# Hybrid decoder layer on one core: squares of the second x tile on two engines, meta rows scaled on GpSimd, third-last write finished on chip

## The chip, the cores and the metric

The kernel runs on 1 core of one Trainium2 chip. The metric is the device time of one execution in microseconds (us); of several executions the median is given. Engine names are those of the profile: PE is TensorE (PEld its weight loads), DVE is VectorE, ACT is ScalarE, POOL is GpSimd, SP is SyncE, which here only issues DMAs.

## What is computed

One decoder layer over 1024 tokens of width 1024, with 16 learned meta tokens in front that are dropped from the output. Cut to what matters here:

```python
def rmsnorm(x, g):
    y = x * lax.rsqrt(jnp.mean(x * x, axis=-1, keepdims=True) + EPS)
    return y * g

h = jnp.concatenate([meta, x], axis=1)          # 16 + 1024 rows of 1024
u = rmsnorm(h, g_pre_mix)
z = u @ w_in                                     # q, k, v and two recurrent inputs
mix = concat([attention(q, k, v), recurrence(xr, yr)]) @ w_out
h = h + rmsnorm(mix, g_post_mix)
u = rmsnorm(h, g_pre_ffn)
f = jnp.square(jax.nn.relu(u @ w_ff1)) @ w_ff2   # D_FF = 4096
h = h + rmsnorm(f, g_post_ffn)
return h[:, N_META:]
```

Everything is float32. The kernel splits each matmul operand into a high and a low part and makes three matmuls of every product (`mm3`, L125, L130 and L131).

## The kernel before

Two ends of the program matter; between them TensorE works on projections, attention, the recurrence and the two feed-forward products.

**The start.** The rows come in tiles of 128. The first block is the 16 meta rows and x tiles 0 and 1 (`xt[0]` and `xt[1]`), 272 rows in all. Each row has to be normalised, transposed on TensorE and split before the first projection (L309) can start. `normed(0)` writes out the order of the work:

- `norm_meta` squares the meta rows on ScalarE (L260); GpSimd adds epsilon (L166) and takes the power -0.5 (L172); VectorE scales the rows (L266).
- `norm_first(xt[0], True)` squares columns 0 to 511 on ScalarE (L235) and 512 to 1023 on VectorE (L242). A square root on ScalarE (L82) and a reciprocal on VectorE (L195) follow (`root_rstd`), then two scalings of 512 columns on VectorE (L248).
- `norm_first(xt[1], False)` squares all 1024 columns on ScalarE (L235), and goes on in the same way.

`transposed_first` then fixes TensorE's order with `turn` (L401): six turns of tile 0 (128 columns each), the gain row `g_r`, six turns of the meta rows, then per 128-column block `kc` the turn of tile 1 and the split into high (ScalarE, L117) and low (VectorE, L118). Blocks 6 and 7 are turned later (L426). Ahead of all this, eleven matmuls on zeros (L339) occupy TensorE.

**Order.** The framework lays out each engine's instructions by priority and by a simulated timeline. `behind(name, ins)` adds an edge that only fixes the order on an engine; `chained(e, ins)` strings the instructions of ScalarE (e = 0) or VectorE (e = 1) together; `scaled[0]`, `last[0]`, `last_lut[0]` and `w_low[0]` hold the names such edges refer to. Buffers are taken from pools by tag; tag `d` has four of 128 x 1024 floats.

**The end.** The last feed-forward product leaves four row tiles (j = 0 to 3) whose second half (`facc["0", j]`, columns 512 to 1023) is ready early and whose first half comes out of TensorE last, tile by tile. `finish_half(j)` does what can be done early: squares of the second half, and for j > 1 its product with the gain; for j = 3 it also loads the residual rows `h` from the output tensor (L1572), where an earlier stage stored them. `finish_late(j, y, parts)` adds the last matmul sums (L1188), squares them (L1543), takes root and reciprocal, scales by the gain (L1589), and writes: tiles 0 to 2 through an accumulating DMA that GpSimd issues (L1595) and that adds the rows to the residual in the output tensor; tile 3 in two column halves, each added to `h` on VectorE (L1616) and stored plainly, one half from SP's queue and one from ScalarE's (L1619). Tile 3's matmuls come in two parts of 256 columns (`parts`).

Of the kernel before, what the change touches and what calls it, by code (L numbers as in the profile page):

```python
# [12 lines left out]
ALU = mybir.AluOpType  # L13
# [24 lines left out]
def hybrid_layer(  # L38
# [152 lines left out]
    def root_rstd(ssq, bias, after=None):  # L191
        sd = small.tile([P, 1], F32, name="sd", tag="sd")
        lut(sd, ssq, AF.Sqrt, bias=bias)
        rs = small.tile([P, 1], F32, name="rs", tag="rs")
        ins = nc.vector.reciprocal(rs, sd).ins  # L195
        if after:
            behind(after, ins)
        return rs


    def load_cols(cols, tag="ws"):
        raw = slot("raw", [P, KC, P])
# [24 lines left out]
    u = [pair("a", [P, TT]) for _ in range(KC)]  # L227
    RMS_SC = 1.0 / math.sqrt(D)

    def norm_first(src, halves):  # L230

        xn = slot("d", [P, D])
        ss = [small.tile([P, 1], F32, name=f"hq{i}", tag=f"hq{i}") for i in range(2)]
        c = slice(0, 512 if halves else D)
        square = nc.scalar.activation(  # L235
            xn[:, c], src[:, c], AF.Square, scale=RMS_SC, accum_out=ss[0]
        ).ins
        if not halves:
            behind(last_lut[0], square)
        if halves:  # L240
            c = slice(512, D)
            nc.vector.tensor_tensor_reduce(  # L242
                out=xn[:, c], in0=src[:, c], in1=src[:, c], scale=RMS_SC * RMS_SC,
                scalar=EPS, op0=ALU.mult, op1=ALU.add, accum_out=ss[1],
            )
        rs = root_rstd(ss[0], ss[1] if halves else eps_col, scaled[0])
        for c in (slice(0, 512), slice(512, D)):
            ins = nc.vector.tensor_scalar(  # L248
                xn[:, c], src[:, c], rs, None, op0=ALU.mult
            ).ins  # L250
        scaled[0] = ins.name
        return xn

    scaled = [None]

# [1 line left out]
    def norm_meta():  # L257
        xn = slot("d", [P, D])
        ssq = small.tile([P, 1], F32, name="ssq", tag="ssq")
        nc.scalar.activation(  # L260
            xn[:NMETA], meta_t[:NMETA], AF.Square, scale=RMS_SC, accum_out=ssq[:NMETA]
        )
        rs = rstd_of([ssq[:NMETA]], NMETA)

        def scale():
            ins = nc.vector.tensor_scalar(  # L266
                xn[:NMETA], meta_t[:NMETA], rs, None, op0=ALU.mult
            ).ins
            behind(scaled[0], ins)
            scaled[0] = ins.name  # L270

        return xn, scale

    def norm_rows(src, link, after=None):
        xn = slot("d", [P, D])
# [72 lines left out]

    def normed(b):
        if b == 0:  # L350
            xm, scale = norm_meta()
            first = norm_first(xt[0], True)
            scale()
            return [(xm, NMETA), (first, P), (norm_first(xt[1], False), P)]
# [41 lines left out]
    def transposed_first(xn):  # L396
        (xm, _), (xa, _), (xb, _) = xn
        n, order = ALL[0][1], [None]

        def turn(dst, src):  # L400
            ins = nc.tensor.transpose(dst, src, ident[: src.shape[0], : src.shape[0]]).ins  # L401
# [48 lines left out]
        return hi, lo_  # L450

    xn = normed(0)
    last[0] = last_lut[0]
# [733 lines left out]
    def combine(dst, x0, x1, op):  # L1187
        return nc.vector.tensor_tensor(dst, x0, x1, op=op).ins  # L1188
# [371 lines left out]
    def finish_half(j):  # L1560
# [16 lines left out]
    def finish_late(j, y, parts):  # L1577
# [3 lines left out]
        for k, c in enumerate(parts):  # L1581
            yield k
            ins = combine(acc[:, c], y[k], acc[:, c], ALU.add)
            if k == 1:
                behind(w_low[0], ins)
            if j < 3:
                rs = root_rstd(squares(y[k], acc[:, c], 0), ssq)
                done_ = COLS[0] if j == 2 else slice(0, D)
                w_low[0] = nc.vector.scalar_tensor_tensor(  # L1589
                    o[:, done_], acc[:, done_], rs, gffn_b[:, done_],  # L1590
                    op0=ALU.mult, op1=ALU.mult,
                ).ins.name
                if j == 2:
                    nc.scalar.activation(o[:, COLS[1]], o[:, COLS[1]], AF.Copy, scale=rs)
                nc.gpsimd.dma_start(out[j * P : (j + 1) * P, :], o, accum_op=ALU.add)  # L1595
                continue
            if k == 0:
                part = squares(y[k], acc[:, c], 0)
                nc.scalar.activation(part, part, AF.Identity, bias=ssq)
# [10 lines left out]
            if k == 1:  # L1610
                behind(w_low[0], ins)
            w_low[0] = ins.name
        if j < 3:
            return
        for c, eng in zip(COLS[::-1], (nc.sync, nc.scalar)):
            w_low[0] = nc.vector.scalar_tensor_tensor(  # L1616
                o[:, c], o[:, c], rs, h[:, c], op0=ALU.mult, op1=ALU.add
            ).ins.name
            eng.dma_start(out[j * P : (j + 1) * P, c], o[:, c])  # L1619

    written = set()

# [95 lines left out]
```

## Time and profile before

| what | value |
|---|---|
| median of 3 runs | 945.62 us (945.26 to 947.6) |
| the profiled execution, its own time | 945.83 us |
| its span, first to last instruction | 944.1 us |
| TensorE matmul busy | 935.1 us, 99% |
| VectorE, ScalarE, GpSimd busy | 663.2, 505.8, 135.3 us |
| DMA traffic | 135.96 MB, mean 144 GB/s |
| chain that ended last | PE 98%, DVE 1% |

The profiled execution's own time is 1.7 us longer than its span, which runs from the first instruction to the last. A row of the order of time gives the start, the length, the engine, the line of the kernel, the operation, output<-input tiles and shapes; what stands in brackets is the engine's idle time ahead and what ended it. A row of a stretch gives its length and then the busy time and the number of instructions of PE, PEld, DVE, ACT and POOL, the granted TensorE clock, the share of the DMA engines and GB/s. In the DMA rows each digit is the busy share of one fortieth of the stretch, in tenths.

### The profile page before, as it was taken

What the parts mean: (1) busy time and instruction counts of PE and PEld (TensorE: products, weight loads), DVE (VectorE), ACT (ScalarE), POOL (GpSimd) and SP (SyncE); (2) the same over time, 40 slices, a digit from 0 to 9 for tenths busy, and PEclk for the clock granted to TensorE, in tenths of its full rate; (3) what the DMA queues carried; (4) which work ended last, traced back from release to release, by engine and by line L of the source; (5) the groups of instructions that cost most, each with busy time, mean ns of one, the idle gap of its engine ahead of it and who ended that gap; (6) DMA issues with size and microseconds to landing.
All of it is one profiled execution on the core that took longest, in us unless ns stands there. A gap on an engine that the chain in (4) does not pass through costs nothing.

```text
span 944.1 us, 12155 instructions
## 1 busy us (share of the span) xinstructions
PE 935.1 (99%) x4562; PEld 780.9 (83%) x4562; DVE 663.2 (70%) x844; ACT 505.8 (54%) x847; POOL 135.3 (14%) x205
## 2 busy tenths in 40 slices
PE   9999999999999999999999999999999999999997
PEld 7999999877888878878888888888888888888885
DVE  7668788789877986755544465477667676779883
ACT  8546765679434854443655575653533443445441
POOL 4104437430021200110000000001121000001201
PEclk9999999999999999999999999999999999999999
DMA  8220011104359768573422374334887756637924
GB/s 274 58 67 23 24 46 45 45 23 146 100 182 290 228 193 287 181 249 129 157 89 90 115 219 119 105 112 114 199 173 173 211 180 190 192 131 208 242 63 90
DMA packets 99622, 135.96 MB, mean 144 GB/s; under 512 B 24358, under 2 KB 63286, under 8 KB 99564
## 3 DMA queue, kind: packets, MB, share of 16 engines
q1 hardware_dynamic: 90220, 109.62, 36.7%
q0 software_dynamic: 8880, 24.19, 12.3%
q10 hardware_dynamic: 464, 1.38, 0.4%
q8 instruction: 36, 0.59, 0.3%
q14 instruction: 22, 0.18, 0.1%
HBM read 113.08 MB, written 21.50 MB: 143 GB/s over the span
## 4 chain that ended last, share of the span: by engine, by line
PE 98%; DVE 1%; DMA 0%; ACT 0%; issue 0%; DVEq 0%; ACTq 0%
PE ps_acc L125 11%; PE ps_acc L130 11%; PE ps_acc L131 11%; PE ps_pt L130 7%; PE ps_pt L125 7%; PE ps_pt L131 7%; PE ps_s L125 6%; PE ps_s L131 6%; PE ps_s L130 6%; PE ps_o L125 5%; PE ps_o L130 5%; PE ps_o L131 5%; PE ps_o L763 2%; PE ps_acc L988 1%; PE ps_acc L309 1%; PE ps_s L693 1%
## 5 line engine op out<-in xcount | busy, mean ns | idle before, releaser
L99 DVE TENSOR_TENSOR ws<-raw,ws 128x1024 fp32r<-128x1024 f32 (+1 forms) x69 | 83.1, 1204 | 73.0 <-PE ps_o L130 23.0
L96 ACT CAST ws<-raw 128x1024 fp32r<-128x1024 f32 (+1 forms) x68 | 69.8, 1026 | 82.9 <-PE ps_o L130 32.8
L96 ACT CAST ws<-e 128x1024 fp32r<-128x1024 f32 x41 | 43.0, 1049 | 85.0 <-PE ps_o L130 37.8
L99 DVE TENSOR_TENSOR b<-b,b 128x1024 fp32r<-128x1024 f32 (+1 forms) x49 | 57.6, 1176 | 27.1 <-PE ps_o L130 21.9
L130 PE MATMUL ps_acc<-a,ws 128*128 128x512 f32 (+3 forms) x224 | 76.3, 341 | 0.0
L125 PE MATMUL ps_acc<-a,ws 128*128 128x512 f32 (+3 forms) x224 | 76.3, 341 | 0.0
L131 PE MATMUL ps_acc<-a,ws 128*128 128x512 f32 (+3 forms) x224 | 75.7, 338 | 0.0
L99 DVE TENSOR_TENSOR ws<-e,ws 128x1024 fp32r<-128x1024 f32 x41 | 50.1, 1223 | 31.4 <-ACT ws L96 18.0
L96 ACT CAST b<-b 128x1024 fp32r<-128x1024 f32 (+1 forms) x49 | 49.6, 1012 | 41.4 <-DVE b L1188 35.3
L750 POOL TENSOR_SCALAR_AFFINE_SELECT c<-c 128x512 fp32r<-128x512 f32 x64 | 53.1, 844 | 73.5 <-ACT c L96 64.5
L131 PE MATMUL ps_acc<-ws,b 128*128 128x512 f32 (+1 forms) x120 | 46.1, 384 | 0.0
L130 PE MATMUL ps_acc<-ws,b 128*128 128x512 f32 (+1 forms) x120 | 46.1, 384 | 0.0
L125 PE MATMUL ps_acc<-ws,b 128*128 128x512 f32 (+1 forms) x120 | 46.0, 385 | 0.0
L125 PEld LDWEIGHTS ps_acc<-a,ws 128*128 128x128 f32 x224 | 42.2, 188 | 3.1 <-DVE b L997 0.3
L131 PEld LDWEIGHTS ps_acc<-a,ws 128*128 128x128 f32 x224 | 42.2, 188 | 3.0
L130 PEld LDWEIGHTS ps_acc<-a,ws 128*128 128x128 f32 x224 | 42.1, 188 | 2.8
L125 PE MATMUL ps_pt<-ws,b 128*128 128x512 f32 x112 | 44.2, 395 | 0.0
L130 PE MATMUL ps_pt<-ws,b 128*128 128x512 f32 x112 | 44.2, 395 | 0.0
L131 PE MATMUL ps_pt<-ws,b 128*128 128x512 f32 x112 | 44.0, 393 | 0.0
L125 PE MATMUL ps_s<-ws,b 128*128 128x512 f32 x110 | 43.5, 395 | 0.0
L130 PE MATMUL ps_s<-ws,b 128*128 128x512 f32 x110 | 43.3, 393 | 0.0
L131 PE MATMUL ps_s<-ws,b 128*128 128x512 f32 x110 | 43.2, 393 | 0.0
(437 smaller groups left out, 2679.9 us busy)
## 6 DMA issues: line engine op xcount, KB each, us to landing
raw<-in_w_ff_dram SPq DMA_DIRECT2D x59, 512.0 KB
e<-in_w_ff_dram SPq DMA_DIRECT2D x43, 512.0 KB
a<-in_w_ff_dram SPq DMA_DIRECT2D x12, 512.0 KB
s_dram<-a POOLq DMA_DIRECT2D x12, 512.0 KB, 3.8
raw<-in_w_in_dram SPq DMA_DIRECT2D x9, 512.0 KB
c<-in_x_dram SPq DMA_DIRECT2D x8, 512.0 KB
d<-in_x_dram SPq DMA_DIRECT2D x8, 512.0 KB
out_dram<-raw SPq DMA_DIRECT2D x8, 512.0 KB
```

Source lines behind the costliest of these rows:

```text
L96: cast[0] = nc.scalar.copy(hi, src).ins.name
L99: low = nc.vector.tensor_tensor(lo, src, f32(hi), op=ALU.subtract).ins
L125: ins = nc.tensor.matmul(dst, lh, rh, start=start, stop=False, skip_group_check=True).ins
L130: nc.tensor.matmul(dst, lh, rl, start=False, stop=False, skip_group_check=True)
L131: last_mm[0] = nc.tensor.matmul(dst, ll, rh, start=False, stop=stop, skip_group_check=True).ins.name
L309: last_mm[0] = nc.tensor.matmul(acc[:, :n], w[k // 2][:, kc, :], u[kc][k % 2][:, t0 : t0 + n], start=k == 0 and kc == 0, stop=k == last an ...
L693: nc.tensor.matmul(dst, q[h][:, c], hi, start=True, stop=False, skip_group_check=True,)
L750: nc.gpsimd.affine_select(out=p_[:, :, s], in_=f32(p_[:, :, 0]), pattern=[[0, 4], [g, P]], compare_op=op, fill=0.0, base=0, channel_multip ...
L763: nc.tensor.matmul(two[:, :, oc : oc + w], v, p_.rearrange("p (j i) s c -> p j (i s c)", j=2)[:, :, pc : pc + w], start=n == 0 and k == 0, ...
L988: ins = nc.tensor.matmul(y2_bank[half], (wh, wh, wl)[k][:, kc, :], (uh, ul, uh)[k][:, t0 : t0 + n], start=m % 24 == 0, stop=m % 24 == 23, ...
```

## The change

At the start, both x tiles are squared in halves on ScalarE and VectorE. VectorE's order becomes: squares of tile 0, its reciprocal, squares of tile 1, scaling of the first half of tile 0, reciprocal of tile 1, scaling of tile 1 in pieces of 256, 256 and 512 columns. ScalarE scales the second half of tile 0. GpSimd scales the meta rows, right behind its power. On TensorE only four blocks of tile 0 and of the meta rows are turned ahead; those of blocks 4 and 5 come with tile 1's.

At the end, tile 2 also loads its residual rows (a second buffer of tag `d`, a second load on SP's queue) and is finished on chip: VectorE multiplies by the gain while the squares run, adds the residual to each half, and SP's queue stores the halves. The store of the first half stands behind the first addition of tile 3. The accumulating DMA of tile 2 and ScalarE's scaling of its second half (L1594) are gone.

```diff
@@ root_rstd
+        roots[0] = ins.name
         return rs
@@
-    def norm_first(src, halves):
+    def squares_first(src):
...
         square = nc.scalar.activation(
             xn[:, c], src[:, c], AF.Square, scale=RMS_SC, accum_out=ss[0]
         ).ins
-        if not halves:
+        if scaled[0]:
             behind(last_lut[0], square)
...
+        c = slice(512, D)
+        ins = nc.vector.tensor_tensor_reduce(
+            out=xn[:, c], in0=src[:, c], in1=src[:, c], scale=RMS_SC * RMS_SC,
+            scalar=EPS, op0=ALU.mult, op1=ALU.add, accum_out=ss[1],
+        ).ins
+        if scaled[0]:
+            behind(scaled[0], ins)
+        scaled[0] = ins.name
+        return xn, ss
+
+    def scale_first(xn, src, rs, *cols):
+        for c in cols:
             ins = nc.vector.tensor_scalar(
                 xn[:, c], src[:, c], rs, None, op0=ALU.mult
             ).ins
+            behind(scaled[0], ins)
+            scaled[0] = ins.name
@@ norm_meta
-        def scale():
-            ins = nc.vector.tensor_scalar(
-                xn[:NMETA], meta_t[:NMETA], rs, None, op0=ALU.mult
-            ).ins
...
+        nc.gpsimd.tensor_scalar(xn[:NMETA], meta_t[:NMETA], rs, None, op0=ALU.mult)
+        return xn
@@ normed
+            xm = norm_meta()
+            xa, sa = squares_first(xt[0])
+            ra = root_rstd(*sa, scaled[0])
+            scaled[0] = roots[0]
+            xb, sb = squares_first(xt[1])
+            scale_first(xa, xt[0], ra, slice(0, 512))
+            rb = root_rstd(*sb, scaled[0])
+            scaled[0] = roots[0]
+            ins = nc.scalar.activation(
+                xa[:, 512:], xt[0][:, 512:], AF.Copy, scale=ra
+            ).ins
+            behind(last_lut[0], ins)
+            last[0] = ins.name
+            scale_first(xb, xt[1], rb, slice(0, 256), slice(256, 512), slice(512, D))
+            return [(xm, NMETA), (xa, P), (xb, P)]
@@ transposed_first
         for kc in range(6):
             pts.append(bank(("o", "s", "pt")[kc % 3]))
-            turn(pts[kc][:, NMETA : NMETA + P], xa[:, cols(kc)])
+            if kc < 4:
+                turn(pts[kc][:, NMETA : NMETA + P], xa[:, cols(kc)])
...
-        for kc in range(6):
+        for kc in range(4):
             turn(pts[kc][:, :NMETA], xm[:NMETA, cols(kc)])
         for kc in range(KC):
             if kc < 6:
                 pt = pts[kc]
+                if kc > 3:
+                    turn(pt[:, NMETA : NMETA + P], xa[:, cols(kc)])
+                    turn(pt[:, :NMETA], xm[:NMETA, cols(kc)])
                 turn(pt[:, NMETA + P : n], xb[:, cols(kc)])
@@ finish_half
-        if j > 2:
+        if j > 1:
             h = slot("d", [P, D])
             nc.sync.dma_start(h, out[j * P : (j + 1) * P, :])
@@ finish_late
+            if j == 2:
+                gained = combine(o[:, c], acc[:, c], gffn_b[:, c], ALU.mult)
+                behind(ins.name, gained)
+                rs = root_rstd(squares(y[k], acc[:, c], 0), ssq, gained.name)
+                write = rows_out(j, o, h, rs)
+                write(COLS[1], nc.sync)
+                continue
...
             if k == 0:
+                behind(w_low[0], ins)
+                w_low[0] = ins.name
+                first_out[0](COLS[0], nc.sync)
                 part = squares(y[k], acc[:, c], 0)
...
+    def rows_out(j, o, h, rs):
+        def write(c, eng):
+            ins = nc.vector.scalar_tensor_tensor(
+                o[:, c], o[:, c], rs, h[:, c], op0=ALU.mult, op1=ALU.add
+            ).ins
...
+            eng.dma_start(out[j * P : (j + 1) * P, c], o[:, c])
```

More of the change, by code (lines that the diff above doesn't have):

```diff
@@ L197, in root_rstd @@
             behind(after, ins)
+        roots[0] = ins.name
         return rs
+    roots = [None]
     def load_cols(cols, tag="ws"):
@@ L228, in hybrid_layer @@
     RMS_SC = 1.0 / math.sqrt(D)
-    def norm_first(src, halves):
+    def squares_first(src):
         xn = slot("d", [P, D])
         ss = [small.tile([P, 1], F32, name=f"hq{i}", tag=f"hq{i}") for i in range(2)]
-        c = slice(0, 512 if halves else D)
+        c = slice(0, 512)
         square = nc.scalar.activation(
@@ L237, in norm_first @@
         ).ins
-        if not halves:
+        if scaled[0]:
             behind(last_lut[0], square)
[L240 to L247, printed above, removed]
+        c = slice(512, D)
[9 more added lines that the diff above has]
+        for c in cols:
             ins = nc.vector.tensor_scalar(
@@ L250, in norm_first @@
             ).ins
-        scaled[0] = ins.name
-        return xn
+            behind(scaled[0], ins)
+            scaled[0] = ins.name
     scaled = [None]
@@ L263, in norm_meta @@
         rs = rstd_of([ssq[:NMETA]], NMETA)
-        def scale():
-            ins = nc.vector.tensor_scalar(
-                xn[:NMETA], meta_t[:NMETA], rs, None, op0=ALU.mult
-            ).ins
-            behind(scaled[0], ins)
-            scaled[0] = ins.name
-        return xn, scale
+        nc.gpsimd.tensor_scalar(xn[:NMETA], meta_t[:NMETA], rs, None, op0=ALU.mult)
+        return xn
     def norm_rows(src, link, after=None):
@@ L452, in hybrid_layer @@
     xn = normed(0)
-    last[0] = last_lut[0]
     rk = fetch([(K_COL, P)], pieces=2)
@@ L1609, in finish_late @@
             ins = combine(o[:, c], acc[:, c], gffn_b[:, c], ALU.mult)
-            if k == 1:
-                behind(w_low[0], ins)
+            behind(w_low[0], ins)
             w_low[0] = ins.name
@@ L1614, in finish_late @@
             return
+        write = rows_out(j, o, h, rs)
         for c, eng in zip(COLS[::-1], (nc.sync, nc.scalar)):
-            w_low[0] = nc.vector.scalar_tensor_tensor(
+            write(c, eng)
+    first_out = [None]
+    def rows_out(j, o, h, rs):
+        def write(c, eng):
+            ins = nc.vector.scalar_tensor_tensor(
                 o[:, c], o[:, c], rs, h[:, c], op0=ALU.mult, op1=ALU.add
-            ).ins.name
+            ).ins
+            if w_low[0]:
+                behind(w_low[0], ins)
+            w_low[0] = ins.name
             eng.dma_start(out[j * P : (j + 1) * P, c], o[:, c])
+        first_out[0] = write
+        return write
     written = set()
```

12 lines of the change are left out of this document (2 added, 10 removed).

## The prediction

> **What bounds the kernel now.** I read the span first, then the busy times by stretch of it, then the order of time in the first 10 us and the last 15 us.
>
> ```profile
> span 944.1 us, 12155 instructions
> ```
>
> ```profile
> 1.50:6.57 5.07, 5.06 (x11) 3.48 (x11) 1.27 (x5) 3.81 (x8) 4.11 (x10) 1.00 0.93 295
> ...
> 11.38:937.18 925.80, 925.71 (x4524) 774.12 (x4522) 654.20 (x821) 497.50 (x828) 129.76 (x187) 1.00 0.49 142
> 937.18:944.10 6.92, 0.00 (x0) 0.00 (x0) 2.83 (x7) 0.20 (x1) 0.40 (x1) 0.85 0.76 166
> ```
>
> The reader should see that TensorE (first figure after the length) works 925.71 of the 925.80 us between 11.38 and 937.18. No edit in there can gain anything. What the change touches is the 11.4 us ahead of that block and the 6.9 us behind it, and a shift of the block passes to the end one to one.
>
> **The start, before.** The rows of TensorE, VectorE, ScalarE and GpSimd in order of time, start and duration in front:
>
> ```profile
> 6.80 0.30 PE L401 MATMUL ps_o<-ident,d 128*128 128x128 f32 x1 [0.22 <-DVE d L248]
> ...
> 7.37 0.27 PE L401 MATMUL ps_pt<-ident,d 128*128 128x128 f32 x1
> 7.58 0.22 PE L401 MATMUL ps_acc<-ident,vmt 8*128 8x8 f32 x1
> ...
> 8.03 0.21 PE L401 MATMUL ps_s<-ident,d 16*128 16x16 f32 x1
> 8.09 0.21 PE L401 MATMUL ps_pt<-ident,d 16*128 16x16 f32 x1
> 8.49 0.30 PE L401 MATMUL ps_o<-ident,d 128*128 128x128 f32 x1 [0.20 <-DVE d L248]
> ...
> 9.43 0.39 PE L309 MATMUL ps_acc<-a,b 128*128 128x272 f32 x1
> ```
>
> ```profile
> 4.84 0.69 DVE L242 CUSTOM_DVE_ANT_0 d<-c 128x512 f32<-128x512 f32 x1 [3.37 <-DMA c<-in_x_dram]
> ...
> 6.17 0.88 DVE L248 TENSOR_SCALAR d<-c,rs 128x512 f32<-128x512 f32 x2
> 6.96 0.73 DVE L266 TENSOR_SCALAR d<-d,rs 16x1024 f32<-16x1024 f32 x1
> ```
>
> ```profile
> 6.07 1.06 ACT L235 ACTIVATE d<-c 128x1024 f32<-128x1024 f32 x1
> ...
> 8.89 0.49 ACT L117 ACTIVATE a<-ps_o,gcol 128x272 fp32r<-128x272 f32 x1 [0.77 <-PE ps_o L401]
> ```
>
> ```profile
> 5.01 0.61 POOL L166 TENSOR_SCALAR ms<-ssq 16x1 f32<-16x1 f32 x1 [0.48 <-ACT d L260]
> 5.71 0.57 POOL L172 TENSOR_TENSOR rs<-ms,half_pow 16x1 f32<-16x1 f32 x1
> ```
>
> The path is: first x tile scaled on VectorE (its two halves from 6.17 take 0.88 and overlap a little, so the first is done about 6.65), TensorE's turns from 6.80, the second x tile scaled, its first turn at 8.49, the split at 8.89, the first projection at 9.43. What comes last there is the second tile, whose square alone holds ScalarE for 1.06 us.
>
> **The start, after.** VectorE's scaling of the meta rows (0.73 at 6.96) leaves it. The square halves: ScalarE squares 512 columns, VectorE the other 512, as it does for the first tile in 0.69 us. But in the new order VectorE squares x tile 1 *before* it scales x tile 0: from 6.07 (x tile 1 has landed, ScalarE read it then) to 6.76. The square is done 0.37 earlier (6.07 + 1.06 = 7.13). The price is that x tile 0's scaling starts at about 6.8 instead of 6.17.
>
> Now GpSimd. Its power ends at 5.71 + 0.57 = 6.28, and with the 0.09 us that lay between its two rows above, the meta scaling asks for SBUF at 6.37, while VectorE's square is under way. What two such neighbours do to each other stands at 81 and 202 us:
>
> ```profile
> 80.61 1.33 DVE L99 TENSOR_TENSOR ws<-raw,ws 128x1024 fp32r<-128x1024 f32 x1
> 81.86 1.13 DVE L788 TENSOR_SCALAR d<-d,prm 128x1040 f32<-128x1040 f32 x1
> ```
>
> ```profile
> 80.82 1.61 POOL L750 TENSOR_SCALAR_AFFINE_SELECT c<-c 128x512 fp32r<-128x512 f32 x1
> ```
>
> ```profile
> 202.11 0.69 DVE L917 COPY c<-c 64x1040 f32<-64x1040 f32 x1
> 202.23 1.48 POOL L916 COPY c<-c 64x1040 f32<-64x1040 f32 x1 [10.50 <-DVE c L915]
> ...
> 202.83 1.98 DVE L881 TENSOR_TENSOR b<-b,b 128x1040 fp32r<-128x1040 f32 x1
> ...
> 204.74 1.23 DVE L918 TENSOR_TENSOR c<-c,d 128x1040 f32<-128x1040 f32 x1
> ```
>
> The same VectorE operation takes 1.23 us alone and 1.98 behind a GpSimd copy; the copy itself ends 0.91 us after VectorE's copy (202.80 to 203.71). They exclude each other, in the order of asking: at 81.94 GpSimd got in although VectorE's scaling had been dispatched at 81.86, and that scaling ended 0.56 us after GpSimd (82.43 to 82.99), 1.13 in all. VectorE's square of x tile 0 holds GpSimd off too: the 16x1 addition at 5.01 ends at 5.62, just behind the square's 5.53. The Trainium skill, "SBUF — State Buffer", section "Who interferes with whom", states that whoever of the two issues first gets a shared pair of ports for the whole instruction and the other fully blocks; the trace agrees, with the 1.98 against 1.23.
>
> So I take: square of x tile 1 to 6.76; GpSimd's scaling of 16x1024 gets in, about 0.9 us (the 1040-column copy's 0.91 is the nearest row; from below VectorE's own 0.73 at 6.96, from above the copy's whole 1.48), to 7.66; only then x tile 0's first half, which needs another 0.3 or so (half of the 0.56): 8.0. TensorE's first turn follows 0.15 later, as 6.80 followed 6.65: **8.15**. Then four turns 0.11 apart (six from 6.80 to 7.37), the g row 0.21 behind the fourth (7.37 to 7.58), four meta turns and x tile 1's first, 0.06 apart (8.03 to 8.09): 8.15 + 0.34 + 0.21 + 5 x 0.06 = 9.0, against 8.49. X tile 1 itself is ready by then: its reciprocal waits behind x tile 0's scaling too (8.1), and a 256-column scaling takes less than the 0.44 of a 512-column one. The split follows 0.40 later (8.49 to 8.89): 9.4. **Start: +0.5 us.** ScalarE's added copy of 512 columns, under the 1.06 of 1024, fits between the end of its square, near 6.8, and the split, where its only other work is a cast and the g column; if that cover went, it would cost up to 0.7. The last four turns of x tile 0 and of the meta rows move between those of x tile 1, where TensorE waits for the splits. Should GpSimd take 1.48, the start is +1.1; if nothing excludes, x tile 0's half is scaled by 7.28, the turns start at 7.43 and x tile 1's at 8.3: -0.2.
>
> **The tail.** Rows of VectorE, the issues, the one DMA queue at work from 938 to 941, and the DMA share in fortieths of 939 to 943:
>
> ```profile
> 935.08 0.43 DVE L1188 TENSOR_TENSOR a<-ps_o,a 128x256 f32<-128x256 f32 x1
> 935.43 0.74 DVE L1589 SCALAR_TENSOR_TENSOR a<-a,rs,ws 128x512 f32<-128x512 f32 x1
> 936.09 0.42 DVE L1188 TENSOR_TENSOR a<-a,ws 128x256 f32<-128x256 f32 x1
> 937.20 0.42 DVE L1188 TENSOR_TENSOR a<-ps_acc,a 128x256 f32<-128x256 f32 x1 [0.70 <-PE ps_acc L131]
> ```
>
> ```profile
> 936.72 0.86 POOL L1595 DMA_DIRECT2D out_dram<-a  x1 [2.90 <-ACT sq L1599]
> ...
> 939.61 0.36 SPq L1619 DMA_DIRECT2D out_dram<-a  x1
> 940.27 0.35 ACTq L1619 DMA_DIRECT2D out_dram<-a  x1
> ```
>
> ```profile
> q0 software_dynamic: 118, 0.48, 102.8%
> ```
>
> ```profile
> DMA  0968988984998989899899269999999999984100
> ```
>
> The accumulating DMA of output tile 2, the third of the four, (q0) fills all engines (102.8%) until the dip at 941.2, where the two last stores begin; these end near 942.8. They were issued at 939.61 and 940.27, so the first one waited about 1.65 us. On idle engines a transfer begins 1.0 us after its issue. Here is one, with the fortieths of the 2 us from 833.65:
>
> ```profile
> 833.65 0.37 SPq L1478 DMA_DIRECT2D raw<-in_w_ff_dram  x1
> ```
>
> ```profile
> DMA  0000000000000000000039959202015299599996
> ```
>
> Without the accumulation the first store starts at 940.6 and all is 0.65 earlier: **tail -0.65 us**. The bounds: nothing, if 1.65 us is a store's own delay; -0.9, if the two, issued 0.66 apart, also no longer wait for each other. GpSimd's 0.86 for that issue goes too, with nothing behind it. That tile's plain stores go out behind two VectorE operations at about 935.7 and 936.7, and 0.25 MB each is through by 939.
>
> VectorE pays for it ahead of 937.20. Its product with g falls into its wait for ScalarE's squares; then from about 935.0 two operations of 0.66 (935.43 to 936.09) and two of 0.35 (935.08 to 935.43) make 937.0. The gate at 937.20 is TensorE's end, so 0.2 us of slack remain; the last tile's squares on ScalarE start 0.6 later, and are needed only behind the addition at 937.20. If that slack is overdrawn, the end moves by as much, some 0.2. The second residual load goes on SP's queue; its buffer comes free with the last reads here, long before 935:
>
> ```profile
> L1188 DVE TENSOR_TENSOR b<-d,a x2: 1224/1224/1225, 831.3 to 841.7; 128x1024 f32<-128x1024 f32 x2
> ```
>
> **Sum.** +0.5 - 0.65 = -0.15: a span of 943.95, 945.7 for the profiled execution (945.83), which lies 0.21 above the median of 945.62. On the median: **945.5**, chance 0.47. This is no change: 0.3%, 2.8 us, is about what a measurement of this kernel can tell.
>
> **Rivals.**
> - *GpSimd does not hold up x tile 0's scaling.* -0.2 - 0.65 = -0.85: 944.8. Against it the 1.13 at 81.86; for it that 16 partitions are a small operation. 0.20.
> - *The tail gains nothing* since the delay is the store's own: 945.62 + 0.5 = 946.1. For it, both stores end about as far behind their issue; against it, the quiet load's 1.0. 0.13.
> - *The clock.* TensorE pauses from 6.57 to 8.15 instead of 6.80. It ran at half rate up to there (11 matmuls of 512 columns in 5.06 us, 0.9 ns a column), and at 0.5 ns a column in the first projections, 34 of 272 columns in 4.76 us:
>
> ```profile
> 11.70 4.76 PE L309 MATMUL ps_acc<-a,b 128*128 128x272 f32 x34
> ```
>
> ```profile
> 941.27:942.01 0.74, 0.00 (x0) 0.00 (x0) 0.00 (x0) 0.00 (x0) 0.00 (x0) 1.00 0.99 365
> 942.01:944.10 2.09, 0.00 (x0) 0.00 (x0) 0.00 (x0) 0.00 (x0) 0.00 (x0) 0.50 0.32 121
> ```
>
>   If the pause brings half rate back, these cost between nothing and 4.8 us more; I take the 2.0 by which one run of before (947.6) lay above the two others: 947.5, slower than before. It decides once the pause outlasts what the clock watches. After the last matmul (937.18) the granted clock stayed 1.00 until 942.01 and was 0.50 then, which speaks against 1.6 us being enough. 0.14. The Trainium skill, "TensorE: Matmul & The Clock Gate", Part 1, has a free-running window of 3413 ns that must be idle as a whole; by that the pause alone would not do it, and no row here shows how a sparsely used window counts.
> - *SP's order*: if the second residual load is queued ahead of weight loads that are due before its buffer is free, the weights stand behind it. It decides from the point where that wait outlasts the lead of the weight loads. The two reads above lie 841.7 - 831.3 = 10.4 us apart; if the load is put one such stretch too early and the lead covers half, TensorE stops for 5: 950.5, slower. TensorE's 925.71 of 925.80 with one such load in the queue speaks against it. 0.06.
>
> **The range** takes in the first four: 944.3 (the 944.8, with the tail's deeper bound and what two of the runs of before differ by, 945.26 and 945.62) to 947.6. Slower by over 0.3% are the last rival, 0.06, and the clock's upper bound, 0.01; faster by that much has no case of its own and gets 0.02 out of the second; the rest is same, 0.91.
>
> **What would show it.** Right: a VectorE scaling of x tile 0 of about 1.2 us instead of under half a us, a GpSimd scaling that ends near 7.7, first projection near 9.95, no q0 traffic behind 939, the last two stores starting 1.0 us after their issue. Wrong: a first projection ahead of 9.43, a pause of TensorE between 12 and 937, 272-column matmuls 0.25 apart instead of 0.125 behind 10, stores that still start 1.65 us late.

## The result and the profile after

The change made the kernel slower: 949.47 us median (948.98 to 949.99, 6 runs) against 945.66 (945.26 to 947.6, 6 runs), a ratio of 1.0041 with a 95% interval from 1.003 to 1.0052. The profiled execution took 949.34 us, its span is 947.4. Before the change the first record of a full TensorE clock stands at 6.76 us, after it at 17.90.

First TensorE of the changed kernel in order of time (start, length, engine, line, operation, tiles, shapes, count; in brackets the idle time ahead and what ended it):

```profile
4.66 1.91 PE L339 MATMUL ps_acc<-ws 128*128 128x512 f32 x4
8.56 0.45 PE L412 MATMUL ps_o<-ident,d 128*128 128x128 f32 x1 [1.99 <-DVE d L254]
8.80 0.42 PE L412 MATMUL ps_s<-ident,d 128*128 128x128 f32 x1
...
9.71 0.26 PE L412 MATMUL ps_o<-ident,d 16*128 16x16 f32 x1
...
10.49 0.42 PE L412 MATMUL ps_s<-ident,d 128*128 128x128 f32 x1
...
12.66 0.80 PE L309 MATMUL ps_acc<-a,b 128*128 128x272 f32 x2
```

The zero-matmuls end at 6.57 as before. The pause behind them is 1.99 us instead of 0.22. The turns are then about 0.21 apart instead of 0.11, so TensorE is at half rate, and the first projection starts at 12.66 instead of 9.43. VectorE and GpSimd beside that:

```profile
7.03 0.98 DVE L243 CUSTOM_DVE_ANT_0 d<-c 128x512 f32<-128x512 f32 x1 [0.74 <-DMA c<-in_x_dram]
7.94 0.08 DVE L243 DVE_READ_ACCUMULATOR2_ANT hq<- 128x1 f32 x1
7.94 0.48 DVE L254 TENSOR_SCALAR d<-c,rs 128x512 f32<-128x512 f32 x1
8.44 0.16 DVE L195 RECIPROCAL rs<-sd 128x1 f32<-128x1 f32 x1
8.64 1.47 DVE L254 TENSOR_SCALAR d<-c,rs 128x256 f32<-128x256 f32 x3
```

```profile
6.36 2.94 POOL L271 TENSOR_SCALAR d<-d,rs 16x1024 f32<-16x1024 f32 x1
```

GpSimd's scaling of 16 meta rows takes 2.94 us, from 6.36 to 9.30. In this execution x tile 1 also landed late: VectorE waited for its DMA until 7.03, while in the other traces of the whole kernel ScalarE reads it from 6.0 to 6.2. As VectorE now squares x tile 1 ahead of scaling x tile 0, the delay passed to the first turn; the pause of 1.99 us here is partly of that making. The same start in an execution without it has a pause of 1.75 (start_only, below).

The stretches of the span (length, then busy time and count of PE, PEld, DVE, ACT and POOL, granted clock, DMA share, GB/s):

```profile
12.66:17.90 5.24, 5.24 (x22) 4.68 (x23) 3.78 (x7) 3.62 (x7) 0.00 (x0) 1.00 1.08 317
17.90:23.14 5.24, 5.24 (x44) 5.24 (x44) 3.71 (x5) 3.78 (x10) 3.45 (x5) 1.00 0.78 298
...
17.90:941.04 923.14, 923.05 (x4512) 772.65 (x4511) 652.99 (x818) 494.05 (x823) 126.80 (x186) 1.00 0.48 141
941.04:947.44 6.40, 0.00 (x0) 0.00 (x0) 2.83 (x7) 0.20 (x1) 0.00 (x0) 0.65 0.49 175
```

The first two rows are of equal length: 22 matmuls up to 17.90, 44 behind it. The clock column says 1.00 in both, because ahead of the first record of a change the view has nothing else to show; there the rate is read from counts and durations. In this execution the clock was not up before 17.90. In the other five runs of the changed kernel the mean granted clock is 0.992 to 0.995, against 0.998 here, and a mean counts half rate only behind the first record: there the clock had come up and fell back, as a trace below shows. The third row shows that the middle is as full as before, and the last that the end took 6.40 us where it took 6.92. Its last stores, their issues and the fortieths of the 4 us from 942 (0.1 us each):

```profile
943.45 0.33 SPq L1648 DMA_DIRECT2D out_dram<-a  x1
```

```profile
944.12 0.35 ACTq L1648 DMA_DIRECT2D out_dram<-a  x1
```

```profile
DMA  9999997742000000000000298999989999996100
```

The queues are empty from about 943.0 to 944.2; the first of the two stores begins 0.8 us after its issue, where before it began 1.65 after. Both kernels issue it 2.41 us behind the last addition's start (937.20 to 939.61, 941.04 to 943.45).

### The profile page after: what moved, and what is told of

Same layout as the page of the kernel before. It is cut to its first block, busy times and chain, and to the rows that moved or that the text cites. A ratio compares the mean times of both kernels' runs of the same rounds, so it can differ in the third digit from the quotient of the medians.

```text
span 947.4 us, 12161 instructions
## 1 busy us (share of the span) xinstructions
PE 937.5 (99%) x4562; PEld 783.8 (83%) x4562; DVE 665.7 (70%) x847; ACT 505.6 (53%) x847; POOL 134.8 (14%) x205
## 4 chain that ended last, share of the span: by engine, by line
PE 98%; DMA 1%; DVE 0%; DVEq 0%; issue 0%; SPq 0%
PE ps_acc L125 11%; PE ps_acc L131 11%; PE ps_acc L130 11%; PE ps_pt L130 7%; PE ps_pt L125 7%; PE ps_pt L131 7%; PE ps_s L125 6%; PE ps_s L131 6%; PE ps_s L130 6%; PE ps_o L125 5%; PE ps_o L130 5%; PE ps_o L131 5%; PE ps_o L777 2%; PE ps_acc L1002 1%; PE ps_acc L309 1%; PE ps_s L707 1%
```

## The experiments

All times are medians with lowest and highest. The kernel before ran beside each group: 945.92 (945.12 to 948.02, 27 runs) beside the first four kernels, 945.66 (944.96 to 948.65, 34 runs) beside the next four, 945.65 (945.08 to 948.35, 35 runs) beside the last four.

**The tail alone, the start alone.** tail_only is the kernel before with the change's edits to `finish_half`, `finish_late` and `rows_out`; start_only is the kernel before with all the other edits, and with its own end. Of tail_only:

```diff
-        if j > 2:
+        if j > 1:
             h = slot("d", [P, D])
...
+            if j == 2:
+                gained = combine(o[:, c], acc[:, c], gffn_b[:, c], ALU.mult)
...
+                write(COLS[1], nc.sync)
+                continue
...
+                first_out[0](COLS[0], nc.sync)
```

Of start_only:

```diff
-            xm, scale = norm_meta()
-            first = norm_first(xt[0], True)
-            scale()
-            return [(xm, NMETA), (first, P), (norm_first(xt[1], False), P)]
+            xm = norm_meta()
+            xa, sa = squares_first(xt[0])
...
+            return [(xm, NMETA), (xa, P), (xb, P)]
```

> The kernel before with the end of the changed one alone. Theory A (the loss is all at the start; the end gained about 0.5 us, read from the span behind VectorE's last addition to the matmul sums: 6.9 us before, 6.4 after): 945.1, about 0.5 under before. Rival (the end gained nothing by itself, the 0.5 comes with the later start): 945.65, as before.

> The changed kernel's start with the end of before. Theory A: all of the loss and none of the gain, 945.65 + 3.8 = 949.5, or up to 950.0 beside the changed kernel's 949.5. Rival (the second residual load or the new stores cost something in the middle or at the end): under 949, nearer to before.

The tail alone: 945.23 (944.86 to 947.3, 11 runs), ratio 0.9992 (0.9983 to 1.0001), 0.69 below its neighbour. That interval just takes in no change, but its trace has the gain too: 6.40 us from the last addition's start (936.60) to the end of the span (943.0). The start alone: 950.54 (949.43 to 950.82, 5 runs), ratio 1.0042 (1.003 to 1.0055), which is 0.5 above the 950.0 allowed and 4.6 above its neighbour. The loss lies wholly in the start. Its stretches, cut where the granted clock changes:

```profile
7.05:10.46 3.41, 1.39 (x11) 1.14 (x12) 3.37 (x6) 1.56 (x4) 3.16 (x2) 1.00 1.20 308
10.46:17.29 6.83, 6.83 (x30) 5.53 (x29) 4.79 (x11) 5.11 (x10) 0.00 (x0) 0.50 1.07 324
17.29:20.70 3.41, 3.41 (x29) 3.41 (x29) 2.64 (x4) 2.32 (x5) 1.88 (x3) 1.00 1.02 412
```

Here the clock had reached full rate at 7.05, TensorE was busy for 1.39 of the next 3.41 us, and at 10.46 the clock fell to half for 6.83 us: 30 matmuls there, 29 in half the time behind it.

**The clock against contention.** The changed kernel with 18 zero-matmuls, which reach to 7.7 and cover most of the pause; and the kernel before with 7, which opens a pause of 1.9 us (4.86 to 6.73) in a start that is otherwise not changed:

```diff
-    load(11, 512)
+    load(18, 512)
```

```diff
-    load(11, 512)
+    load(7, 512)
```

> The changed kernel with 18 instead of 11 matmuls on zeros ahead of the first turn, so that TensorE has no pause of 2 us. Clock theory (the pause leaves TensorE at half rate until 17.9 us instead of 6.8, and most of the 3.8 us comes of that): full rate from about 7 us, 947.5 or less. Contention theory (GpSimd's scaling of 2.9 us and what it holds up make the loss, the clock little): 949.4, or later by what the extra matmuls delay the first turn.

> The kernel before with 7 instead of 11 matmuls on zeros, so that TensorE pauses from about 4.9 to 6.8 us, as the changed kernel does from 6.6 to 8.6. Clock theory: half rate up to 10 us or later, 947.5 to 949. Contention theory: nothing else has changed, 945.65.

The first took 946.91 (946.51 to 948.65, 11 runs; 1.001, 1.0002 to 1.0019), 2.56 below the changed kernel. The second took 947.86 (947.08 to 948.63, 11 runs; 1.0018, 1.0009 to 1.0027), with nothing else changed than that TensorE stops earlier. In its profiled execution half rate lasted until 16.26, as the counts show (44 matmuls in 9.53 us, then 40 in 4.74):

```profile
6.73:16.26 9.53, 9.53 (x44) 8.58 (x45) 7.96 (x17) 7.54 (x16) 0.30 (x1) 1.00 1.09 299
16.26:21.00 4.74, 4.74 (x40) 4.74 (x40) 3.13 (x5) 2.95 (x10) 3.35 (x5) 1.00 0.98 390
```

So the pause costs by itself, through the clock, and most of the loss is this. What is left, 946.91 with a tail that gives 0.69, is another 1.7 us of start. The 18 zero-matmuls do not keep the clock in every execution: seven of the eleven runs took 946.51 to 947.0 and four 947.82 to 948.65. The profiled one is among the four (948.33): its pause is 0.79 us, and it fell to half rate for 3.41 us.

```profile
8.84:12.25 3.41, 2.68 (x21) 1.85 (x19) 2.76 (x6) 1.66 (x5) 1.51 (x2) 1.00 1.13 301
12.25:15.66 3.41, 3.41 (x16) 3.10 (x16) 2.89 (x7) 2.81 (x7) 0.00 (x0) 0.50 1.16 333
```

Ahead of that fall it shows what GpSimd does in the changed start when x tile 1 is there in time. VectorE's scaling of x tile 0 takes 1.33 us instead of under half a us, and TensorE's first turn of the meta rows waits for GpSimd's end:

```profile
6.41 3.52 POOL L271 TENSOR_SCALAR d<-d,rs 16x1024 f32<-16x1024 f32 x1
```

```profile
6.99 1.33 DVE L254 TENSOR_SCALAR d<-c,rs 128x512 f32<-128x512 f32 x1
```

```profile
9.98 0.23 PE L412 MATMUL ps_o<-ident,d 16*128 16x16 f32 x1 [0.73 <-POOL d L271]
```

**GpSimd against the new order.** The changed kernel with the meta rows scaled on VectorE, behind x tile 0's first half; the same with 15 zero-matmuls; and the kernel before with the meta scaling on GpSimd alone:

```diff
-        nc.gpsimd.tensor_scalar(xn[:NMETA], meta_t[:NMETA], rs, None, op0=ALU.mult)
-        return xn
+        def scale():
+            ins = nc.vector.tensor_scalar(
+                xn[:NMETA], meta_t[:NMETA], rs, None, op0=ALU.mult
+            ).ins
+            behind(scaled[0], ins)
+            scaled[0] = ins.name
+
+        return xn, scale
...
             scale_first(xa, xt[0], ra, slice(0, 512))
+            scale()
```

The second has `load(15, 512)` besides. The third, on the kernel before:

```diff
-        def scale():
...
-        return xn, scale
+        nc.gpsimd.tensor_scalar(xn[:NMETA], meta_t[:NMETA], rs, None, op0=ALU.mult)
+        return xn
...
-            scale()
```

> The change with one part undone: the meta rows are scaled on VectorE again, right behind x tile 0's first half; squares on two engines, VectorE's new order and the new tail stay. Theory (GpSimd's long scaling is the first cause: it holds up VectorE's scaling of x tile 0 and, through the meta rows' turns, x tile 1's turns, and the pause then costs the clock): the first turn comes at 7.4 to 7.6 instead of 8.5, the first projection at 9.8 to 10.2 with a full clock, and the time is 945.4 to 946.8, the upper end where the pause of 0.9 us still costs the clock. Rival (VectorE's new order, x tile 1's square ahead of x tile 0's scaling, is the first cause): first turn still at 8 or later, 948.5 or more.

> As the kernel before it in this call, with 15 instead of 11 zero-matmuls ahead of the first turn, so that TensorE does not pause there. Theory: 945.2 to 945.8 (a start some 0.3 us later than in the kernel before the change, a tail 0.7 shorter), below the 946.9 of the change with 18 zero-matmuls by about the 1.2 us that GpSimd's scaling costs beside the clock. Rival (new order is the first cause): 946.7 to 947.1, as with 18 zero-matmuls and GpSimd.

> The kernel before the change with one part of the change alone: the 16x1024 meta scaling on GpSimd; squares, VectorE's order, turns and tail as before. Theory: GpSimd takes about 3 us beside VectorE, from 6.4 to 9.3 or later; the meta rows' turns wait for it, x tile 1's stand behind them, the first projection comes at 10.5 to 11: 946.8 to 947.5 with a full clock, up to 949 if the pause of TensorE costs the clock. Rival (GpSimd's scaling lies beside the path, the new order of VectorE is the cause): first projection by 9.7, 945.7 to 946.2.

With 15 zero-matmuls: 945.4 (944.86 to 946.4, 12 runs; 0.9994, 0.9985 to 1.0002), as the theory has it and 1.51 below the 946.91 with GpSimd (1.25 when each is taken against its own neighbour). TensorE's rows:

```profile
7.35 0.30 PE L419 MATMUL ps_o<-ident,d 128*128 128x128 f32 x1 [0.41 <-DVE d L254]
...
9.91 0.49 PE L315 MATMUL ps_acc<-a,b 128*128 128x272 f32 x2
```

With 11: 946.94, just above the 946.8 that the theory allowed, and no typical run. The twelve are 944.73 to 945.22 five times and 946.56 to 949.27 seven times: one start that keeps the clock in some executions and loses it in the others. The five have a mean granted clock of 0.998 or 0.999, six of the seven 0.995 to 0.997. The profiled execution is one of the five (945.22); its clock was full from 4.60 on, and it stayed full over a pause of 1.71 us:

```profile
7.43 0.30 PE L419 MATMUL ps_o<-ident,d 128*128 128x128 f32 x1 [1.71 <-DVE d L254]
```

```profile
4.60:8.01 3.41, 1.70 (x10) 1.00 (x8) 2.58 (x8) 3.20 (x10) 0.92 (x2) 1.00 1.06 341
8.01:11.42 3.41, 3.33 (x25) 2.51 (x25) 3.32 (x9) 2.92 (x9) 0.26 (x1) 1.00 1.22 314
```

GpSimd's scaling alone, in the old order: 948.83 (947.17 to 950.98, 11 runs; 1.0029, 1.002 to 1.0039). That is above the 946.8 to 947.5 expected with a full clock and inside what was allowed with a lost one. TensorE, GpSimd and VectorE there:

```profile
9.45 0.23 PE L394 MATMUL ps_o<-ident,d 16*128 16x16 f32 x1 [0.88 <-POOL d L265]
...
10.89 0.98 PE L303 MATMUL ps_acc<-a,b 128*128 128x272 f32 x2
```

```profile
6.32 3.08 POOL L265 TENSOR_SCALAR d<-d,rs 16x1024 f32<-16x1024 f32 x1
```

```profile
6.18 1.75 DVE L248 TENSOR_SCALAR d<-c,rs 128x512 f32<-128x512 f32 x2
...
8.03 1.65 DVE L248 TENSOR_SCALAR d<-c,rs 128x512 f32<-128x512 f32 x2
```

The meta rows' first turn waits for GpSimd (0.88 <-POOL), and VectorE's two pairs of scalings take 1.75 and 1.65 where they took 0.88 and 0.93. The stretches by clock:

```profile
7.48:10.89 3.41, 2.22 (x18) 1.44 (x17) 2.61 (x6) 1.36 (x5) 2.34 (x2) 1.00 1.19 314
10.89:17.72 6.83, 6.83 (x28) 6.19 (x29) 6.33 (x11) 6.25 (x12) 0.42 (x1) 0.50 1.05 337
```

**What the scaling costs by itself.** A kernel of nothing but such operations, each alone between barriers, then beside VectorE or ScalarE (M is 16, `g` GpSimd, `v` VectorE, `hold` the barrier; the helper at L94 that makes the 16x1024 scaling is written out here):

```diff
+    g.tensor_scalar(one[:M], meta_t[:M], rs[:M], None, op0=ALU.mult)
+    hold()
...
+    g.tensor_scalar(one[:M, :512], meta_t[:M, :512], rs[:M], None, op0=ALU.mult)
+    hold()
+    g.tensor_scalar(one, meta_t, rs, None, op0=ALU.mult)
+    hold()
...
+    g.tensor_copy(one[:M], meta_t[:M])
+    hold()
+    g.tensor_scalar(one[:M], meta_t[:M], rs[:M], None, op0=ALU.mult)
+    for c in (slice(0, 512), slice(512, D)) * 4:
+        v.tensor_scalar(two[:, c], xa[:, c], rs, None, op0=ALU.mult)
+    hold()
```

> Leaves the whole computation out (the output is a scaled copy of one x tile): GpSimd's scaling of 16 rows x 1024 by a column of factors alone (twice), with 512 columns, with 128 rows, with a constant factor, as a plain copy; then beside a chain of eight VectorE scalings of 128x512, beside four VectorE squares of 128x512, and beside eight ScalarE scalings of 128x512. Theory (GpSimd and VectorE take turns at a shared resource): about 1.8 us alone and beside ScalarE, 2.8 to 3.5 beside VectorE, whose own operations grow too. Rival (GpSimd is slow at this operation by itself): 2.8 to 3.0 alone and beside each of them.

GpSimd and VectorE in order of time:

```profile
7.24 2.83 POOL L94 TENSOR_SCALAR d<-c,rs 16x1024 f32<-16x1024 f32 x1 [0.21 <-SPq L97]
10.28 1.55 POOL L103 TENSOR_SCALAR d<-c,rs 16x512 f32<-16x512 f32 x1 [0.21 <-SPq L97]
12.04 2.84 POOL L105 TENSOR_SCALAR d<-c,rs 128x1024 f32<-128x1024 f32 x1 [0.21 <-SPq L97]
...
18.03 1.03 POOL L109 COPY d<-c 16x1024 f32<-16x1024 f32 x1 [0.19 <-SPq L97]
19.27 3.66 POOL L94 TENSOR_SCALAR d<-c,rs 16x1024 f32<-16x1024 f32 x1 [0.21 <-SPq L97]
...
31.47 2.83 POOL L94 TENSOR_SCALAR d<-c,rs 16x1024 f32<-16x1024 f32 x1 [0.49 <-SPq L97]
```

```profile
19.20 4.80 DVE L113 TENSOR_SCALAR d<-c,rs 128x512 f32<-128x512 f32 x8 [18.36 <-SPq L97]
24.14 3.26 DVE L116 TENSOR_SCALAR d<-c,rs 128x512 f32<-128x512 f32 x8
```

My theory of that moment, 1.8 us alone and the rest from VectorE, fell: the scaling takes 2.83 us alone, 2.50 ns a column ((2.83 - 1.55) / 512), with 16 rows as with 128, while a copy of the same size takes 1.03. Beside ScalarE, whose scalings overlap 1.63 us of it, it stays 2.83. The rival, slow by itself and beside each of them alike, holds only in part: beside VectorE's scalings it takes 3.66, and these take 4.80 instead of 3.26. Beside four VectorE squares it takes 3.38, and one of the squares 1.48 instead of 0.69. This kernel ran once.

**By which way GpSimd reaches the path.** The changed kernel with 18 zero-matmuls and GpSimd's scaling in two halves; TensorE's first four meta turns read the first half only:

```diff
-        nc.gpsimd.tensor_scalar(xn[:NMETA], meta_t[:NMETA], rs, None, op0=ALU.mult)
+        for c in (slice(0, 512), slice(512, D)):
+            nc.gpsimd.tensor_scalar(
+                xn[:NMETA, c], meta_t[:NMETA, c], rs, None, op0=ALU.mult
+            )
```

> The change with 18 zero-matmuls (946.9) and GpSimd's meta scaling cut into two instructions of 512 columns, 1.55 us each by the measurement alone. TensorE's first four turns of the meta rows read the first half only. Theory (the meta rows' turns, which stand in TensorE's order ahead of x tile 1's, wait for the end of GpSimd's long instruction): they start near 9.0 instead of 9.98, the first split near 9.8 instead of 10.70, the time is 945.9 to 946.3. Rival (it is VectorE's scaling, lengthened by GpSimd, that comes last): the first split does not move by more than 0.2, 946.7 to 947.1.

946.07 (945.88 to 947.03, 11 runs), 0.84 below the undivided one, or 0.57 when each is taken against its own neighbour: the theory's value. The first meta turn is at 8.83 (9.98 undivided), the first split at 9.58 (10.76), and now the second half is what TensorE waits for, briefly:

```profile
10.10 0.49 PE L415 MATMUL ps_s<-ident,d 16*128 16x16 f32 x2 [0.18 <-POOL d L272]
```

Not all of the gain is the turns'. The cut shortened VectorE's scaling of x tile 0 too (0.91 us instead of 1.33), which brought the first turn to 8.22 instead of 8.47: 0.25 of the 1.18 by which the first split is earlier. And part may be the clock: none of these runs lies as high as the four late ones of the undivided kernel. The other 0.67, down to the 945.4 without GpSimd, holds VectorE's lengthened scalings and this second wait; no run divides it further.

**Length of the pause or place of the window.**

The kernel before with two zero-matmuls less:

```diff
-    load(11, 512)
+    load(9, 512)
```

> The kernel before the change with 9 zero-matmuls instead of 11, so that TensorE pauses about 1.1 us ahead of its first turn (0.23 with 11, 1.9 with 7). Theory by phase (the loss depends on where the free-running window of 3.4 us falls, and a longer pause spoils more of its places): a part of the runs at 945.2 to 946.0 as with 11, the rest at 947 to 949, median between 945.7 and 947.9. Rival (a threshold in the length of the pause): all runs at one level, either that with 11 (945.7) or that with 7 (947.9).

Of twelve runs two took 945.2 and 945.93 and ten 948.18 to 949.0; nothing between. The same program costs nothing in some executions and about 3 us in the others. The part that loses is larger than I had thought: the median, 948.79, lies above the 947.9 allowed, and above the 947.86 of the kernel with seven zero-matmuls, whose pause is longer. The profiled execution is one of the two; the pause was 0.99 us, and the clock held:

```profile
5.87:9.28 3.41, 2.34 (x19) 1.85 (x19) 3.03 (x8) 2.50 (x7) 0.49 (x2) 1.00 1.14 322
9.28:12.69 3.41, 3.35 (x18) 2.49 (x19) 3.37 (x9) 3.41 (x9) 0.00 (x0) 1.00 1.08 298
```

The pauses of the other eleven are not recorded. By the traces of this start, where the first turn stands at 6.71 to 6.99 and nine zero-matmuls at half rate end near 5.7, they are some 1.0 to 1.3 us (an estimate). A threshold in the length does not fit that: a pause of 1.71 us kept the clock (meta_dve), and an execution without any pause over 0.79 us lost it (after_warm). The busy time of a window does not decide either: half rate followed 2.68 us of work in 3.41 there and did not follow 1.70 in meta_dve. What differs from execution to execution is where the clock first comes up: in twelve traces it is anywhere from 4.60 to 7.51 us, although the zero-matmuls start at 1.51 or 1.52 in each. That fits a window whose place differs from run to run.

**Versions that the answers point to.** Zero-matmuls put between the first turns of the kernel with the new tail; the changed kernel with x tile 0 scaled first and no work on GpSimd; and the new tail with one zero-matmul more:

```diff
         turn(pg[:, :8], g_r)
+        order[0] = load(2, 256, order[0])
...
             turn(pts[kc][:, :NMETA], xm[:NMETA, cols(kc)])
+        order[0] = load(3, 256, order[0])
...
                 turn(pt[:, NMETA + P : n], xb[:, cols(kc)])
+                if kc == 5:
+                    order[0] = load(3, 256, order[0])
```

```diff
-            xb, sb = squares_first(xt[1])
             scale_first(xa, xt[0], ra, slice(0, 512))
+            xb, sb = squares_first(xt[1])
             scale()
```

```diff
-    load(11, 512)
+    load(12, 512)
```

> The kernel before the change with the new tail, and eight zero-matmuls of 256 columns put between the first turns (two behind the g row's, three behind the meta rows', three behind x tile 1's), where TensorE waits for VectorE and ScalarE. Theory (a stretch in which TensorE works little can throw the clock back, by where the 3.4 us window falls, which differs from run to run): fewer late runs, none of them above 946.5, median 944.9 to 945.2. Rival (the spread of the runs has another cause): the spread stays, some runs in ten above 946.5, median 945.2 to 945.6 or later by what the zero-matmuls hold up.

> The change with the meta rows scaled on VectorE and x tile 0's first half scaled ahead of x tile 1's square, as before the change; the squares of x tile 1 on two engines, ScalarE's copy and the new tail stay. Theory: first turn at 6.8 as before the change, so no pause and no loss of clock in more runs than before; x tile 1 ready at most 0.2 later; 944.9 to 945.5. Rival (each reordering of the start costs more than the tail gives): 945.7 to 946.5.

> The kernel before the change with the new tail (945.2 to 945.9) and 12 instead of 11 zero-matmuls. Theory: without the last 0.2 us of pause fewer runs fall back to half the clock: median 944.9 to 945.2, no more than one run in ten above 946.5. Rival (the late runs come from the sparse stretch behind the first turns, which this does not touch): as the new tail alone, 945.2, with some in ten above 946.5.

The bridged kernel: 945.73 (945.31 to 946.92, 12 runs; 0.9998, 0.9989 to 1.0006). Two of its runs lie above 946.5, where the theory had none, and its first split came at 9.77 instead of 9.00 with the new tail alone, so the zero-matmuls themselves held up the turns. It decides nothing.

With x tile 0 first: 947.32 (945.0 to 948.06, 12 runs; 1.0007, 0.9997 to 1.0016). My theory fell: five runs stood at 945.0 to 945.51, as expected, and seven at 947.28 to 948.06, although the pause was only 0.39 us in the profiled run, one of the five. The five have a mean granted clock of 0.998 or 0.999 and the seven 0.994 to 0.996, so it is the clock again that was lost. Whether the pause or the changed turns behind it did this, the runs do not tell.

The new tail with 12 zero-matmuls: 945.17 (944.83 to 945.71, 11 runs; 0.999, 0.9981 to 0.9998). None of its runs lies above 946.5, where 11 of the 35 runs of the kernel before beside it do. It is below both kernels, by 0.48 us and by 4.3. That the twelfth zero-matmul adds to the new tail is not shown: 945.17 and 945.23 are too near.

## Why the prediction was wrong

The forecast was 945.5 and the time is 949.47, outside the range and on the side of the rival on the clock. The step that failed is the start term: +0.5 us in the sum, +3.84 in the trace (the last addition starts at 941.04 instead of 937.20). Two things in it were wrong: GpSimd's scaling was put at 0.9 us and takes 2.83 or more, and the pause's effect on the clock, the larger part, stood at nothing in the sum and only among the rivals.

- **What bounds the kernel: right.** TensorE works 923.05 of the 923.14 us between 17.90 and 941.04, and what the start loses passes to the end. That also takes SP's order out: no stall in the middle.
- **VectorE's new order: gains nothing, and one agreement is luck.** With the meta rows back on VectorE and most of the pause filled (meta_dve_warm), the first turn comes at 7.35, near the 7.43 that the prediction had without GpSimd in the way, and the first split at 8.86, against 8.89 before. The first projection at 9.91 looks like the predicted 9.95, but that figure contained GpSimd's delay. It comes 1.05 us behind the first split instead of 0.54, for the turns of blocks 4 and 5 now stand ahead of it on TensorE; the prediction put them at nothing. The time shows little of this: 945.4 against the 945.23 of the tail alone.
- **GpSimd's scaling: wrong size, and one way not seen.** 0.9 us, bounded by 1.48 at most, was 2.94, and 2.83 alone. The estimate came from a copy; the copy measured here takes 1.03 and the scaling 2.83. The one row that the prediction quoted of a GpSimd operation that computes, 1.61 us for 512 columns, scales to 3.2 for 1024, but by luck: it is one of 64 such operations in the kernel before, and their median is 0.635. No row of before prices the scaling. The prediction let GpSimd act only through VectorE, on x tile 0. It acted through TensorE's order too: the meta rows' turns stand ahead of x tile 1's and wait for GpSimd's end. Together 1.25 to 1.5 us. Cutting the scaling in two gives 0.57 to 0.84 of that back, by the traces mostly through the turns.
- **Exclusion: right in kind, wrong in detail.** The sign that the prediction named, a scaling of x tile 0 of about 1.2 us, shows in after_warm and start_only with 1.33. In the profiled execution of the changed kernel, where x tile 1 landed late, it took 0.48, as without a neighbour, in the middle of GpSimd's 2.94 us. In after_warm the 1.33 us end at 8.32, while GpSimd goes on to 9.93. The prediction, with the Trainium skill's "SBUF — State Buffer", section "Who interferes with whom", had GpSimd hold VectorE off for the whole instruction; the page says this of VectorE's two-port modes, and no row shows the mode here. The traces do not agree with a hold over the whole instruction: the neighbour cost VectorE 1.54 us of GpSimd's 3.66 in the measurement by itself.
- **The clock: the mechanism was named, and weighed wrongly.** It was given 0.14 and 2.0 us. It costs 2.56 (949.47 against 946.91), 2.82 with each against its own neighbour, and all six runs of the change pay it. What spoke against it was the end of the trace, where the clock stayed full for 4.8 us behind the last matmul. That shows how long the clock can stay up, not how short a pause can bring it down: ten of twelve runs of before_9, with two zero-matmuls less, lost some 3 us. The Trainium skill's "TensorE: Matmul & The Clock Gate", Part 1, as the prediction read it, wants a window idle as a whole; start_only went to half rate behind a window with 1.39 us of work in 3.41. On the free-running window the traces agree: the changes at the start of start_only, meta_gps and after_warm lie 3.41 us or twice that apart. What share or kind of work holds a window up stays open, since a window with 2.68 us of work was followed by half rate in after_warm and one with 1.70 was not in meta_dve.
- **The tail: right.** -0.65 in the sum, -0.52 in the traces (6.92 to 6.40, in the changed kernel and with the tail alone) and -0.69 in the medians of the tail alone. The two last stores begin 0.8 us after issue instead of 1.65, and their packets end about 4.8 us behind the last addition's start instead of 5.6, by the DMA rows (945.8 and 942.8). From there to the end it is 1.6 us instead of 1.3, which gives part of it back; why, no run shows. VectorE's slack held: its last addition ahead of the gate ends at 940.90, 0.14 us before 941.04.

```profile
940.48 0.42 DVE L1202 TENSOR_TENSOR a<-a,ws 128x256 f32<-128x256 f32 x1
941.04 0.42 DVE L1202 TENSOR_TENSOR a<-ps_acc,a 128x256 f32<-128x256 f32 x1
```

The sum with what was measured, each kernel against its own neighbour: -0.69 for the tail, +0.43 for the order, +1.25 for GpSimd, +2.82 for the clock, +3.81 in all. These are the steps from tail_only over meta_dve_warm and after_warm to the change, so they add up by construction and do not check one another, and the number of zero-matmuls differs between them (11, 15, 18, 11). Without the neighbours they are -0.69, +0.17, +1.51 and +2.56.

## What to carry to other kernels

Price an operation by the same operation on the same engine; where there is no row of it, time it alone, as gps_bench did, and take a copy as a lower bound only. When work moves to a slower engine, follow its result to the first reader and look at what is queued behind that reader. Where TensorE is warmed up by hand, a reordering that opens a pause of a microsecond ahead of the real work cost many executions here some 3 us, so fill the pause again and look at the spread of the runs, not at the median alone.

## What the runs showed of the hardware

- GpSimd's scaling of f32 columns by a factor: 2.83 us for 1024 columns, 1.55 for 512, the same for 16 and 128 rows, 2.76 with a constant factor; a copy 1.03.
- Beside VectorE the 1024 columns took from 2.94 to 3.66 us, beside ScalarE, with 1.63 us of overlap, 2.83.
- The median hides the clock: the same kernel gave 945.2 and 949.0 (before_9), 945.0 and 948.06 (x0_first), 944.73 and 949.27 (meta_dve), in groups with gaps of over 1.3 us between them.
- One execution kept the full clock over a pause of TensorE of 1.71 us (meta_dve), and another lost it without a pause over 0.79 us (after_warm).
- With zero-matmuls from 1.51 us on, the first record of the full clock stands anywhere from 4.60 (meta_dve) to 7.51 us (x0_first).
